# A hybrid encoder layer on one core: FFN blocks stored in two halves, squares through PSUM, the last norm rearranged

## Chip, core and metric

The kernel runs on one core of a Trainium2 chip. The metric is device time in microseconds (us) of one execution; the time before is the median of three runs. A core has TensorE (PE in the profile, its weight loads PEld), VectorE (DVE), ScalarE (ACT), GpSimd (POOL) and the queue of SyncE (SP), on which this kernel issues its DMAs.

## The reference

One layer over 1024 tokens (and 16 meta tokens) of width 1024, all in float32. The mixer is not touched by the change; what follows it is:

```python
def _rmsnorm(x, w):
    y = xf * lax.rsqrt(jnp.mean(xf * xf, axis=-1, keepdims=True) + RMS_EPS)
    return (y * w).astype(x.dtype)

def _swiglu(u, w_gate, w_up, w_down):
    return (jax.nn.silu(u @ w_gate) * (u @ w_up)) @ w_down

    for l in range(DEPTH):
        h = h + _mixer(_rmsnorm(h, norm_mix_w[l]), ...)
        h = h + _swiglu(_rmsnorm(h, norm_ffn_w[l]), w_ffn_gate[l], w_ffn_up[l], w_ffn_down[l])
    h = _rmsnorm(h, norm_final_w)
    return h[:, N_META:]
```

The FFN has 2816 hidden features, 11 blocks of 256.

## The kernel before

Activations lie with features on the 128 partitions and tokens along the free dimension, in tiles of 128 x 512 float32 (`slot`). A product of two float32 tiles is made of three matmuls on rounded halves: `split` has ACT cast a tile to its high half (L153) and DVE subtract that from the tile for the low half (L154); then come high x high, high x low, low x high.

Large products go through `seven` (L183): a 2 x 2 block product with seven block products instead of eight. It loads four weight pieces a11, a21, a22, a12, has POOL form their sums (L191 to L193, L207), splits each of the seven combinations as it is needed (ACT L209, DVE L210) and accumulates in a PSUM bank (matmuls on L217). The seven are worked in the order 11, t2, t3, n1, 21, t4, 22; of the weights, 11, t2, t3 and n1 need the first three pieces, 21 needs a12, and 22 needs a12 taken from t2's sum (L207). `seven_out` (L229) reads the banks: ACT takes the first (L233), DVE the others (L234 to L242).

The stages that matter here, in their order:

1. Output projection (L1208 to L1247), for two token halves c and eight feature tiles m: 24 matmuls, DVE adds the input (L1216), ACT squares the sum (L1245) and POOL adds the squares up in `ssum[c]` (L1246). In the second half the seven combinations for the FFN are formed as well (POOL's difference is L1236). After each half `norm` sums `ssum` over partitions with small matmuls (L1197), takes square root (ACT, L1201) and reciprocal (DVE, L1202) and spreads the factor over partitions by matmul (L174) and an ACT copy to `rs2_b` (L177).
2. Gate and up, 11 blocks j: two `seven` products, 84 matmuls each. Gate results are scaled by `rs2_b` (DVE L1257, POOL L1260 and L1262) and go through Silu (L1261); up results are multiplied in (L1267). For j < 9 the four result tiles are combined to seven (POOL L1282 and L1283, DVE L1284 and L1285), and the seven are stored to `f_d` in DRAM, on SP's queue. Blocks 9 and 10 are stored as they are. For j = 0 three quarters of the first four products are made ahead.
3. Down projection, three groups g of three blocks each (DG = 3, DQ = 3): the 21 tiles of a group are loaded to `xr` (L1303) and split into 42 tiles of the pool `bt`, which holds 58. Then four `seven` products (j = 0 to 3) of 7 x 9 = 63 matmuls each, with weights `w_dq`.
4. The rest of the down projection as plain products with blocks 9 and 10, in token chunks of 512, 256 and 256; the last `norm` of each chunk; `finish` multiplies the eight result tiles by `rs2_b` (L1339; DVE five, POOL three) and stores them.

The order of instructions on each engine is made when the program is built, by a scheduler of the framework from the dependences and its own estimates; each engine, and the SP queue, then works in that order, and a DMA or an instruction that has to wait holds up what stands behind it. A tile of a pool is given out again when its last reader is done.

## Time and profile before

| | us |
|---|---|
| median of three runs | 1775.89 (1775.68 to 1776.03) |
| the profiled execution | 1780.81 |
| its span, first to last instruction | 1779.0 |
| TensorE busy | 1714.6, 8804 matmuls |
| DVE busy | 1339.0 |
| ACT busy | 861.1 |
| POOL busy | 790.1 |
| mean granted TensorE clock | 0.987 of full speed |

The span is that of the profiled execution, which took 4.9 us longer than the median run; times in the views count from the span's start. Matmuls are pipelined and their ends are modelled, so a matmul shows 0.39 us while one begins every 0.23. Idle time of an engine stands in brackets ahead of what ended it.

### The profile page before, as it was taken

The page shows a single profiled execution, that of the slowest core. Times are in us where ns is not written, and L with a number is a line of the kernel's source. Part 1 is how long each engine was busy: PE and PEld are TensorE (multiplying, and loading weights), DVE is VectorE, ACT ScalarE, POOL GpSimd, SP SyncE. Part 2 cuts the span into 40 slices and gives each one's busy share as a digit, 9 for nine tenths or more (in the row PEclk, how much of TensorE's full clock was granted, in tenths as well). Part 3 has the DMA queues.
Part 4 walks back from the last instruction along what each step waited for, and adds up shares of the span by engine and source line. Part 5 has one row for each costly group of instructions (what it writes and reads, how often), then busy time and mean ns, then how long its engine had stood idle before and what let it go on. Part 6 is the DMA issues. An engine that isn't in the chain of part 4 may idle for free.

```text
span 1779.0 us, 26433 instructions
## 1 busy us (share of the span) xinstructions
PE 1714.6 (96%) x8804; PEld 1443.9 (81%) x8804; DVE 1339.0 (75%) x2448; ACT 861.1 (48%) x1614; POOL 790.1 (44%) x605
## 2 busy tenths in 40 slices
PE   8999999999999899999999999899999999999997
PEld 6788777788887677899998888788888888787787
DVE  7845778788888857888888758767666666987965
ACT  7425766344324523788787346433332232543434
POOL 1322257674554321234332524666676566533422
PEclk9999999999999899999999999999999999999999
DMA  7733823566546785111112754233323333854512
GB/s 255 240 101 119 295 85 117 180 201 213 189 158 230 213 301 179 28 34 40 30 59 69 231 187 162 66 101 119 101 95 101 107 105 101 286 176 123 154 57 95
DMA packets 145433, 253.59 MB, mean 143 GB/s; under 512 B 18889, under 2 KB 36738, under 8 KB 145298
## 3 DMA queue, kind: packets, MB, share of 16 engines
q1 hardware_dynamic: 145298, 251.92, 43.5%
q8 instruction: 69, 1.13, 0.3%
q14 instruction: 66, 0.54, 0.1%
HBM read 174.93 MB, written 76.85 MB: 142 GB/s over the span
## 4 chain that ended last, share of the span: by engine, by line
PE 49%; DVE 7%; DMA 3%; ACT 3%; issue 2%; SPq 0%; POOL 0%; DVEq 0%; ACTq 0%; POOLq 0%
PE mm L217 29%; PE o L1041 3%; PE mm L138 3%; PE mm L137 3%; PE mm L139 3%; PE t L1012 2%; DVE slot L154 2%; PE s L137 1%; PE s L138 1%; PE s L139 1%; DMA slot<-g_d 1%; DMA slot<-f_d 1%; DVE slot L210 1%; DVE ptl L1015 1%; PE o L137 1%
## 5 line engine op out<-in xcount | busy, mean ns | idle before, releaser
L217 PE MATMUL mm<-slot,slot 128*128 128x512 f32 x2604 | 598.3, 392 | 8.4 <-ACT slot L209 3.7
L217 PEld LDWEIGHTS mm<-slot,slot 128*128 128x128 f32 x2604 | 490.6, 189 | 115.0 <-DVE slot L210 5.5
L209 ACT CAST slot<-slot 128x512 fp32r<-128x512 f32 (+1 forms) x413 | 246.1, 598 | 465.9 <-PE mm L217 395.0
L210 DVE TENSOR_TENSOR slot<-slot,slot 128x512 fp32r<-128x512 f32 (+1 forms) x413 | 361.6, 877 | 71.5 <-ACT slot L209 70.4
L217 PE MATMUL mm<-ht,slot 128*128 128x512 f32 x648 | 219.6, 400 | 7.4 <-DVE slot L210 3.4
L217 PE MATMUL mm<-h,slot 128*128 128x512 f32 x536 | 184.4, 403 | 0.0
L191 POOL TENSOR_TENSOR slot<-slot,slot 128x512 f32<-128x512 f32 (+1 forms) x61 | 85.3, 1398 | 220.0 <-DMA slot<-in_w_u 50.7
L207 POOL TENSOR_TENSOR slot<-slot,slot 128x512 f32<-128x512 f32 (+1 forms) x61 | 84.7, 1390 | 185.1 <-DVE slot L210 173.1
L217 PEld LDWEIGHTS mm<-ht,slot 128*128 128x128 f32 x648 | 122.1, 190 | 35.1 <-DVE slot L210 5.6
L154 DVE TENSOR_TENSOR slot<-slot,slot 128x512 fp32r<-128x512 f32 x137 | 117.5, 872 | 20.6 <-ACT slot L153 20.0
L217 PE MATMUL mm<-lt,slot 128*128 128x512 f32 x324 | 128.7, 397 | 0.0
L153 ACT CAST slot<-slot 128x512 fp32r<-128x512 f32 x137 | 83.3, 619 | 76.9 <-DMA slot<-f_d 30.3
L192 POOL TENSOR_TENSOR slot<-slot,slot 128x512 f32<-128x512 f32 (+1 forms) x61 | 86.0, 1410 | 77.6 <-DVE slot L210 65.6
L217 PEld LDWEIGHTS mm<-h,slot 128*128 128x128 f32 x536 | 101.2, 190 | 21.6 <-DVE slot L210 0.6
L1002 DVE TENSOR_SCALAR_CACHE_REDUCE pr<-s,sq_c 128x384 f32<-128x384 f32 (+1 forms) x192 | 103.3, 573 | 7.9 <-PE t L1020 3.8
L217 PE MATMUL mm<-l,slot 128*128 128x512 f32 x268 | 106.6, 398 | 0.0
L139 PE MATMUL mm<-slot,slot 128*128 128x512 f32 (+1 forms) x288 | 105.3, 366 | 0.0
L138 PE MATMUL mm<-slot,slot 128*128 128x512 f32 (+1 forms) x288 | 105.3, 366 | 0.0
L137 PE MATMUL mm<-slot,slot 128*128 128x512 f32 (+1 forms) x288 | 105.1, 367 | 0.0
L1015 DVE TENSOR_TENSOR ptl<-t,pth 128x512 fp32r<-128x512 f32 x128 | 85.7, 685 | 18.2 <-ACT pth L1014 17.6
L1046 POOL TENSOR_TENSOR oa<-oa,ob 64x256 f32<-64x256 f32 x32 | 24.0, 751 | 154.5 <-ACT ob L1045 149.1
L193 POOL TENSOR_TENSOR slot<-slot,slot 128x512 f32<-128x512 f32 (+1 forms) x61 | 88.2, 1445 | 1.4
(365 smaller groups left out, 3506.0 us busy)
## 6 DMA issues: line engine op xcount, KB each, us to landing
slot<-in_w_in SPq DMA_DIRECT2D x106, 256.0 KB
f_d<-slot SPq DMA_DIRECT2D x71, 256.0 KB
slot<-f_d SPq DMA_DIRECT2D x71, 256.0 KB
slot<-in_xT SPq DMA_DIRECT2D x48, 256.0 KB
slot<-z_d SPq DMA_DIRECT2D x44, 256.0 KB
slot<-in_w_g SPq DMA_DIRECT2D x44, 256.0 KB
slot<-in_w_u SPq DMA_DIRECT2D x44, 256.0 KB
slot<-in_w_dq SPq DMA_DIRECT2D x48, 192.0 KB
```

The lines of the kernel that those rows point to most:

```text
L137: pe.matmul(ps, sh, mh, start=start, stop=False)
L138: pe.matmul(ps, sh, ml, start=False, stop=False)
L139: pe.matmul(ps, sl, mh, start=False, stop=stop)
L154: dve.tensor_sub(lo, t, f(hi))
L191: pool.tensor_add(s1, a21, a22)
L192: pool.tensor_sub(s2, s1, a11)
L193: pool.tensor_sub(a21, a21, a11)
L209: act.copy(hi, side[b])
L210: dve.tensor_sub(low, side[b], f(hi))
L217: pe.matmul(ps, sw[:, ks], sx, start=begins and q == qs[0] and i == 0, stop=q == nq - 1 and i == 2, skip_group_check=True)
L1002: dve.tensor_scalar(pr[:, c], ps[:, :n], sq_c[:, qb : qb + 1], None, ALU.mult, ALU.max, accum_out=mx[:, j : j + 1])
L1015: dve.tensor_sub(pt[1][d], tp, f(pt[0])[d])
```

## The change

- `f_d` for blocks 3 to 8 holds the high halves, and a new DRAM tensor `fl_d` the low ones: in the gate and up part each of the seven tiles is cast (ACT) and subtracted (DVE, in place), and both halves are stored. Groups 1 and 2 of the down projection load the halves straight into `bt` tiles; nothing is split there. Group 0 is as before.
- In the output projection the squares go to a PSUM tile and DVE adds them up; the one difference that POOL made in the second half is DVE's.
- `norm` of the first half stands behind both halves; that of the second half behind the matmuls of the FFN that are made ahead. `seven` remembers what was made ahead.
- `norm` also returns the reciprocal's instruction and the PSUM tile that holds the spread factor. In the last chunk the six products on DVE read that tile instead of `rs2_b`, and POOL has two products instead of three. `finish` of the chunk before is issued in two parts. From the second chunk on, odd tiles are stored from ACT's queue, even ones from SP's.

```diff
+    fl_d = mk(dram, (DQ * (DG - 1), 7, P, 512), "fl_d")
...
-            done = act.copy(dst[:, s0 : s0 + w], ps[:, :w])
-        return done
+            act.copy(dst[:, s0 : s0 + w], ps[:, :w])
+        return ps
...
-            dve.reciprocal(r2c[:, bs], r2c[:, bs])
-            spread(pr_, "r3", rs2_b, r2c, list(bl))
+            done = dve.reciprocal(r2c[:, bs], r2c[:, bs])
+            return done, spread(pr_, "r3", rs2_b, r2c, list(bl))
...
-                    pool.tensor_sub(g12, g12, g22)
+                    dve.tensor_sub(g12, g12, g22)
...
-                    t = slot(xr)
+                    t = mk(pm, (P, 512), "mm")
                     act.square(t, hm)
-                    pool.tensor_add(ssum[c], ssum[c], t)
-            norm(c, slice(0, 512))
+                    dve.tensor_add(ssum[c], t, ssum[c])
+        norm(0, slice(0, 512))
...
                 for b in NAMES[:4]:
                     prod(b, range(3))
-                    rest[b] = range(3, 4)
+                norm(1, slice(0, 512))
...
+                if j < DQ:
+                    for i, t in ((1, t2), (2, v12), (3, n1), (5, t4)):
+                        store(f_d[j, i], t)
+                else:
+                    for i, t in enumerate((v11, t2, v12, n1, v21, t4, v22)):
+                        hi = slot(hr, F32R)
+                        act.copy(hi, t)
+                        dve.tensor_sub(t, t, f(hi))
+                        store(f_d[j, i], f(hi))
+                        store(fl_d[j - DQ, i], t)
...
+                    if g == 0:
+                        raw = slot(xr)
+                        load(raw, f_d[q, i])
+                        blocks[q][nm] = split(raw, bt, bt)
+                        continue
+                    blocks[q][nm] = slot(bt, F32R), slot(bt, F32R)
+                    for t, d in zip(blocks[q][nm], (f_d[g * DQ + q, i], fl_d[(g - 1) * DQ + q, i])):
+                        load(f(t), d)
...
-        def finish(lo, n):
+        def finish(lo, n, factor, some=range(KT)):
...
-                (pool if i in (2, 5, 7) else dve).tensor_mul(hm, hm, rb)
-                store(out[i, :, lo : lo + n], hm)
+                if i in ((5, 7) if last else (2, 5, 7)):
+                    pool.tensor_mul(hm, hm, rb)
+                else:
+                    dve.tensor_mul(hm, factor[:, :n] if last else rb, hm)
+                (nc.scalar.dma_start if lo and i % 2 else store)(out[i, :, lo : lo + n], hm)
...
                 if prev:
                     with tc.issue_after(added.ins):
-                        finish(*prev)
+                        finish(*prev, range(4))
+                    with tc.issue_after(inverse.ins if lo + n == S else added.ins):
+                        finish(*prev, range(4, KT))
```

Three places of the order that results. First PE at the entry to the FFN (L217 before and L220 now are matmuls of the first gate product, L1197 and L1200 the column sums of `ssum[1]`), before and then now:

```order
L217 MATMUL mm_12503<-slot_12241,slot_12505 128x512
L217 MATMUL mm_12461<-slot_11888,slot_12462 128x512
L217 MATMUL mm_12461<-slot_11889,slot_12462 128x512
L217 MATMUL mm_12461<-slot_11888,slot_12463 128x512
L217 MATMUL mm_12475<-slot_12414,slot_12476 128x512
L217 MATMUL mm_12475<-slot_12415,slot_12476 128x512
L217 MATMUL mm_12475<-slot_12414,slot_12477 128x512
L1197 MATMUL r_2788_12435<-ones_68,ssum_2447_11114 128x1 x4
L217 MATMUL mm_12489<-slot_12419,slot_12490 128x512
```

```order
L220 MATMUL mm_12491<-slot_12229,slot_12493 128x512
L1200 MATMUL r_2807_12505<-ones_68,ssum_2448_11115 128x1 x4
L220 MATMUL mm_12449<-slot_11889,slot_12450 128x512
L220 MATMUL mm_12449<-slot_11890,slot_12450 128x512
L220 MATMUL mm_12449<-slot_11889,slot_12451 128x512
L220 MATMUL mm_12463<-slot_12402,slot_12464 128x512
```

The column sums stand right behind the 36 matmuls made ahead, where 42 stood ahead of them before.

Second DVE in the gate and up part, at the end of one of the blocks 3 to 8 and the gate of the next one (L210 and L213 are weight subtractions, L234 to L236 and L237 to L239 evacuations of the gate's banks, L1297 the new subtractions), before and then now:

```order
L1285 TENSOR_TENSOR slot_13981<-slot_13794,slot_13980 128x512
L210 TENSOR_TENSOR slot_14105<-slot_13995,slot_14104 128x512
L235 TENSOR_TENSOR slot_14007<-mm_14044,slot_14006 128x512
L210 TENSOR_TENSOR slot_14126<-slot_14002,slot_14125 128x512
L236 TENSOR_TENSOR slot_14007<-slot_14007,mm_14062 128x512
```

```order
L1289 TENSOR_TENSOR slot_14010<-slot_13823,slot_14009 128x512
L213 TENSOR_TENSOR slot_14162<-slot_14052,slot_14161 128x512
L1297 TENSOR_TENSOR slot_13819<-slot_13819,slot_14015 128x512
L1297 TENSOR_TENSOR slot_14009<-slot_14009,slot_14020 128x512
L1297 TENSOR_TENSOR slot_13726<-slot_13726,slot_14025 128x512
L238 TENSOR_TENSOR slot_14064<-mm_14101,slot_14063 128x512
L1297 TENSOR_TENSOR slot_14008<-slot_14008,slot_14030 128x512
L1297 TENSOR_TENSOR slot_13823<-slot_13823,slot_14035 128x512
L1297 TENSOR_TENSOR slot_14010<-slot_14010,slot_14040 128x512
L1297 TENSOR_TENSOR slot_13727<-slot_13727,slot_14045 128x512
L213 TENSOR_TENSOR slot_14183<-slot_14059,slot_14182 128x512
L239 TENSOR_TENSOR slot_14064<-slot_14064,mm_14119 128x512
```

The seven stand ahead of the weight subtraction for the gate's product 22 and of the evacuation that frees the bank for it.

Third SP's queue in the down projection, at the loads for group 1 (L189 and L190 load weight pieces from `w_dq`, L1303 tiles to be split, L1321 halves), before, from the third to the fourth piece of the group's first product and on to the next product's, and then now, at the fourth piece:

```order
L189 DMA slot_16589<-in_w_dq 128x384
L1303 DMA slot_16533<-f_d_98 128x512
L1303 DMA slot_16539<-f_d_98 128x512
L189 DMA slot_16590<-in_w_dq 128x384
L1303 DMA slot_16545<-f_d_98 128x512
L1303 DMA slot_16551<-f_d_98 128x512
L189 DMA slot_16703<-in_w_dq 128x384
```

```order
L1321 DMA slot_16706<-f_d_98 128x512
L1321 DMA slot_16707<-fl_d_99 128x512
L1321 DMA slot_16710<-f_d_98 128x512
L1321 DMA slot_16711<-fl_d_99 128x512
L190 DMA slot_16717<-in_w_dq 128x384
L190 DMA slot_16830<-in_w_dq 128x384
L190 DMA slot_16831<-in_w_dq 128x384
```

Of the 42 loads of halves for a group, 16 stand among earlier work, and 26 stand together ahead of that fourth piece (`slot_16717`); the pieces of the next product follow it.

## Rows read from the trace of the kernel before

**Rows 1.** The page's first part: engine, busy us, share of the span, instructions.
```profile
PE 1714.6 (96%) x8804; PEld 1443.9 (81%) x8804; DVE 1339.0 (75%) x2448; ACT 861.1 (48%) x1614; POOL 790.1 (44%) x605
```

**Rows 2.** Timeline of PE at the FFN's entry: start, us, what, xcount, [idle before].
```profile
1108.39 4.70 PE L217 MATMUL mm<-slot,slot 128*128 128x512 f32 x20
1115.17 5.30 PE L217 MATMUL mm<-slot,slot 128*128 128x512 f32 x22 [2.08 <-DVE slot L210]
1123.28 1.59 PE L1197 MATMUL r<-ones,ssum 128*128 128x1 f32 x8 [2.80 <-POOL ssum L1246]
1124.73 7.01 PE L217 MATMUL mm<-slot,slot 128*128 128x512 f32 x18
```

**Rows 3.** Windows: us, PE, PEld, DVE, ACT, POOL busy, PEclk, DMA share, GB/s.
```profile
1124.00:1130.00 6.00, 6.00 (x17) 4.84 (x17) 6.00 (x8) 2.61 (x6) 2.60 (x2) 0.50 0.13 44
...
1132.00:1516.00 384.00, 384.00 (x1698) 318.15 (x1697) 259.10 (x310) 122.70 (x205) 252.98 (x171) 1.00 0.32 103
...
1612.00:1616.00 4.00, 3.69 (x11) 2.96 (x12) 4.00 (x8) 1.58 (x4) 0.00 (x0) 0.61 0.82 251
```

**Rows 4.** Timeline of PE from the FFN's end through the down projection's three groups.
```profile
1379.81 152.71 PE L217 MATMUL mm<-slot,slot 128*128 128x512 f32 x673
1533.21 13.05 PE L217 MATMUL mm<-slot,slot 128*128 128x512 f32 x53 [0.70 <-DVE slot L235]
1547.24 6.50 PE L217 MATMUL mm<-slot,slot 128*128 128x512 f32 x27 [0.98 <-DVE slot L210]
1554.11 55.14 PE L217 MATMUL mm<-slot,slot 128*128 128x512 f32 x241 [0.37 <-DVE slot L210]
1612.31 58.93 PE L217 MATMUL mm<-slot,slot 128*128 128x512 f32 x252 [3.06 <-ACT slot L209]
1671.91 0.73 PE L217 MATMUL mm<-slot,slot 128*128 128x512 f32 x2 [0.67 <-ACT slot L209]
1673.06 44.74 PE L217 MATMUL mm<-slot,slot 128*128 128x512 f32 x196 [0.41 <-DVE slot L1321]
```

**Rows 5.** Timeline of DVE at the FFN's entry.
```profile
1112.76 1.76 DVE L154 TENSOR_TENSOR slot<-slot,slot 128x512 fp32r<-128x512 f32 x1
1114.44 0.68 DVE L210 TENSOR_TENSOR slot<-slot,slot 128x512 fp32r<-128x512 f32 x1
...
1115.64 0.68 DVE L1216 TENSOR_TENSOR slot<-mm,slot 128x512 f32<-128x512 f32 x1
```

**Rows 6.** Timeline of POOL at the FFN's entry.
```profile
1112.24 1.72 POOL L1246 TENSOR_TENSOR ssum<-ssum,slot 128x512 f32<-128x512 f32 x1
...
1120.29 1.71 POOL L1236 TENSOR_TENSOR slot<-slot,slot 128x512 f32<-128x512 f32 x1
```

**Rows 7.** Timeline of DVE at the end of one FFN block, j = 4.
```profile
1315.66 1.76 DVE L1284 TENSOR_TENSOR slot<-slot,slot 128x512 f32<-128x512 f32 x1 [1.18 <-POOL slot L1282]
...
1320.26 0.68 DVE L210 TENSOR_TENSOR slot<-slot,slot 128x512 fp32r<-128x512 f32 x1
1320.86 0.67 DVE L236 TENSOR_TENSOR slot<-slot,mm 128x512 f32<-128x512 f32 x1
...
1325.83 0.69 DVE L240 TENSOR_TENSOR slot<-mm,slot 128x512 f32<-128x512 f32 x1
```

**Rows 8.** Timeline of POOL in the same block.
```profile
1321.61 1.67 POOL L1260 TENSOR_TENSOR slot<-slot,rs_b 128x512 f32<-128x512 f32 x1 [3.03 <-DVE slot L236]
```

**Rows 9.** Windows with many loads, columns as in rows 3.
```profile
8.00:24.00 16.00, 15.39 (x56) 12.50 (x57) 10.75 (x17) 11.69 (x20) 0.00 (x0) 1.00 1.04 382
1516.00:1520.00 4.00, 4.00 (x19) 3.30 (x18) 3.77 (x5) 1.77 (x3) 4.00 (x3) 1.00 0.97 326
```

**Rows 10.** Chain of waits, one load in group 1: start, us, what.
```profile
1608.50 2.76 DMA slot<-f_d
```

**Rows 11.** Timeline of DVE and of SP at the end.
```profile
1771.36 3.35 DVE L1339 TENSOR_TENSOR slot<-slot,rs_b 128x256 f32<-128x256 f32 x5 [1.21 <-ACT rs_b L177]
...
1774.40 1.79 SPq L1340 DMA_DIRECT2D out_y<-slot  x4
```

More of the change, by code (lines that the diff above doesn't have):

```diff
@@ L194, in seven @@
         side = {"11": a11, "t2": s2, "t3": a21, "n1": s1, "21": a12, "t4": a22, "22": s2}
-        banks, w, begun = {}, {}, []
+        banks, w, begun, done = {}, {}, [], set()
         def prod(b, qs=range(nq)):
             k = BANK[b]
+            qs = [q for q in qs if (b, q) not in done]
+            done.update((b, q) for q in qs)
             begins = k not in banks
@@ L1278, in build @@
                 n1, t2, t4 = [slot(hr) for _ in range(3)]
-                store(f_d[j, 0], v11)
-                store(f_d[j, 4], v21)
-                store(f_d[j, 6], v22)
+                if j < DQ:
+                    store(f_d[j, 0], v11)
+                    store(f_d[j, 4], v21)
+                    store(f_d[j, 6], v22)
                 pool.tensor_sub(n1, v11, v12)
@@ L1285, in build @@
                 dve.tensor_sub(t4, v21, t2)
-                for i, t in ((1, t2), (2, v12), (3, n1), (5, t4)):
-                    store(f_d[j, i], t)
+                if j < DQ:
+                    for i, t in ((1, t2), (2, v12), (3, n1), (5, t4)):
[7 more added lines that the diff above has]
+                        store(fl_d[j - DQ, i], t)
             else:
@@ L1301, in build @@
                 for q in range(DQ):
-                    raw = slot(xr)
-                    load(raw, f_d[g * DQ + q, i])
-                    blocks[q][nm] = split(raw, bt, bt)
+                    if g == 0:
[6 more added lines that the diff above has]
+                        load(f(t), d)
             for j in range(4):
@@ L1332, in build @@
         acc = [[acc5[m // 2]["21" if m % 2 else "11"], acc5[m // 2]["V" if m % 2 else "12"]] for m in range(KT)]
-        def finish(lo, n):
+        def finish(lo, n, factor, some=range(KT)):
             c, cs = lo // 512, slice(lo % 512, lo % 512 + n)
             rb = rs2_b[:, lo : lo + n]
-            for i in range(KT):
+            last = lo + n == S
+            for i in some:
                 hm = acc[i][c][:, cs]
-                (pool if i in (2, 5, 7) else dve).tensor_mul(hm, hm, rb)
-                store(out[i, :, lo : lo + n], hm)
+                if i in ((5, 7) if last else (2, 5, 7)):
[3 more added lines that the diff above has]
+                (nc.scalar.dma_start if lo and i % 2 else store)(out[i, :, lo : lo + n], hm)
         hid = []
```

4 lines of the change are left out of this document (2 added, 2 removed).

## The prediction

> **What bounds the kernel now.** I read the page's engine shares first. TensorE is busy 96% of the span [rows 1], so time can only come from the places where it stands or runs slowly, and the change leaves its 8804 matmuls as they are. I then went along its timeline from where the change begins, the entry into the FFN. The reader is to see three kinds of loss there.
>
> At the entry, TensorE finishes the output projection, runs 20 matmuls of the first gate block, stands 2.08 us, runs 22 more, and stands 2.80 us for the sum of squares that POOL adds up [rows 2]. Right behind that the granted clock is 0.50, the lower of its two levels (1.2 and 2.4 GHz), from 1124 to 1130 us [rows 3], and 18 matmuls take 7.01 us [rows 2]. At full clock 673 matmuls take 152.71 us [rows 4], 0.227 us each, so 18 should take 4.1: another 2.9 lost. **The entry loses 2.08 + 2.80 + 2.9 = 7.8 us.**
>
> The gate and up part runs without a gap: 384 us busy of 384 [rows 3]. In the down projection, group 0 stands three times, 0.70 + 0.98 + 0.37 = 2.05 us; group 1 stands 3.06 us in its first 40 or so matmuls; group 2 stands 0.67 + 0.41 = 1.08 us [rows 4]. After the 3.06 us the clock falls again: 11 matmuls in 3.69 us [rows 3] instead of 2.5, 1.2 us more. Groups 1 and 2 together lose 3.06 + 1.2 + 1.08 = 5.3 us.
>
> The third is the tail. The last products on DVE begin at 1771.36 and last 3.35 us, and four output stores are issued after that, until 1774.40 + 1.79 = 1776.19 [rows 11]; the span ends at 1779.0.
>
> **Entry: squares through PSUM, and no POOL.** The last projection tile is done when the gate's first matmul starts, at 1108.39 [rows 2], but DVE reads it at 1115.64: it is 7.2 us behind [rows 5]. Its operations with two SBUF inputs take 0.68 us, and 1.76 beside one of POOL's [rows 5, 6]. The change removes 18 POOL operations (14 sums, 4 differences) and puts 18 on DVE. Each costs DVE about 0.68, against the roughly 1.1 it lost to a POOL neighbour. So DVE's queue gets no longer, and by this exchange some 0.4 shorter for each; from the seven or eight in the last four column blocks I take 3 us, and the last tile is read near 1112.6 instead of 1115.64.
>
> From there four steps lead to the complete sum: scaling on ACT, then three adds on DVE, about 3.2 us. That gives 1115.8. TensorE needs it after 36 matmuls, at 1108.39 + 36 x 0.227 = 1116.6. (The sum's matmuls stand 6 earlier than before, by the order on PE above, and the difference that gated the rest at 1120.29 [rows 6] is now a 0.68 on DVE.) So neither stand remains, and without a stand nothing lowers the clock. The margin is under 1 us. I take 7.0 of the 7.8; the bounds are 7.8 and 3, the latter if the sum is still 2 us late and the clock falls as it did.
>
> **FFN blocks stored as two halves.** For six blocks (j = 3 to 8) ACT gets 7 casts, DVE 7 subtractions, SP 7 more stores. TensorE has no slack here, so what counts is who waits. DVE now works the seven ahead of a weight subtraction that stood at 1320.26 and of the evacuation that stood at 1320.86 [rows 7]; the order on DVE above shows both places. TensorE needs both when the product before has ended, which is when DVE could read it, at 1325.83 [rows 7]. The slack is 1325.8 - 1320.94 = 4.9 us. POOL's next operation waits for that same evacuation (1321.61, after 3.03 idle) [rows 8], so POOL is quiet during the seven; they follow each other every 0.6 us (1320.26, 1320.86) [rows 7], 7 x 0.61 = 4.3 us. That just fits. I take 0.1 us per block, **0.6 us lost**; bounds 0 and, at 0.88 each (between the undisturbed 0.68 and the 1.76 of a disturbed one [rows 7]), 6 x (6.2 - 4.9) = 7.8. On SP the weight load behind the stores slips by some 2.8 us. Those weights are split more than 5 us later, so I count nothing; if that cover were gone, the 2.8 would show once per block.
>
> **Down projection.** Group 0 is still split on arrival. Its waits were for DVE and ACT, which in group 0 also split group 1's blocks; these 21 splits go. I take 1.0 of 2.05 (bounds 0 and 2.05). In groups 1 and 2 the 42 splits that made DVE late go altogether. What is late next is the load. A group has 42 tiles, the pool holds 58, so 16 can come early and 26 come while the group before does its last quarter. By the order on SP above, the fourth weight piece of the new group, which its fifth product needs, stands behind all 26 on that queue, where before it stood between the raw loads.
>
> I count from the start of that quarter. 26 loads of 262 KB and two weight pieces of 197 KB are 7.21 MB. The queue moved 382 GB/s for 16 us when it was never empty [rows 9]; that gives 18.9 us. With 0.7 us to the first free tile and 2.0 us for a load's fixed part (2.76 for one [rows 10], less its transfer), the piece lands at 21.6. Cast and subtraction add 1.4 (twice 0.68), so 23.0. The fifth product is due after 63 + 36 matmuls, 22.5. So each group stands 0.5 us instead of losing 4.3 and 1.1: 5.3 - 1.0 = **4.3 us gained**. The upper bound is 5.3 (no stand). For the lower one take the 326 GB/s that the same kind of load had at 1516 to 1520 [rows 9]: 22.1 us of transfer, 3.7 us of standing, and 1.2 for the clock, in each group; 5.3 - 9.8 = -4.5. I take 382 since that stretch is long and its queue is full. The Trainium skill's page "DMA: Bandwidth & Descriptors", section Specifications, gives about 358 GB/s of HBM for a core; a stretch at 382 is above it, but by 358 the transfer would take an estimated 20.1 us, each group would stand 1.7, and the sum would be 2.4 smaller.
>
> **Tail.** Three edits act on one chain. The last reciprocal waits for three products instead of five, but ACT now issues two stores ahead of the square root, so I count nothing for it. The products read the factor in PSUM, not the copy for which DVE stood 1.21 us [rows 11]; the copy is 0.4 of that. They come to 6 on DVE; with a PSUM operand they should not be slowed by POOL, 6 x 0.35 = 2.1 instead of 3.35. The last product ends 1.6 us earlier. Of the four stores that trail it by 1.49, two remain on each queue, which saves about 0.8. **2.4 us**; bounds 0.4 (the copy alone) and 3.3.
>
> **Sum.** 7.0 - 0.6 + 1.0 + 4.3 + 2.4 = 14.1 us. The profiled execution took 1780.81, 4.9 above the median of the runs, 1775.89; it would come to 1766.7, and the median to **1761.8**.
>
> **Rivals.**
> *Late weights* (0.20). Both groups stand 3.7 and lose 1.2 to the clock: 9.8 instead of 1.0, so 1770.6. For it: the weight piece really stands behind 26 loads, and many stretches moved less than 382. Against it: those stretches had a queue that waited for DVE. The skill's page, with 358, would fall between this and the forecast.
> *The entry still waits* (0.12). POOL's four first gate operations slow DVE as before, the sum is 2 us late, the clock falls: 3 instead of 7.0, 1765.8. Against it: the margin is there on paper; for it: it is under 1 us.
> *Slower* (0.06). The seven subtractions run beside POOL at 1.76 [rows 7]: 12.3 us against a slack of 4.9, so TensorE stands 7.4 us in each of six blocks, 44 us, 1806. The forecast turns into a loss when one costs more than (4.9 + 14.7 / 6) / 7 = 1.05 us. Against it: POOL's next operation waits for what stands behind them.
>
> **How the numbers follow.** The forecast has 0.62; its own range is 1757 to 1768. A measurement of this kernel can tell about 0.2%, 3.6 us, from no change, so faster means under 1772.3. The forecast and the waiting entry lie below it, and most of the late weights: 0.62 + 0.11 + 0.14 = 0.87. No change takes 0.07, from late weights with a slow FFN; slower 0.06. The range reaches from 1756.5 to 1771, which leaves out the slow FFN and the edge of the late weights.
>
> **What would show it.** Right: no stand over 1 us around the FFN's entry and clock 1.00 there; no stand in the six blocks over 0.3 us; under 1 us in each of groups 1 and 2, and where it is, a wait for a weight cast behind DMA; the last product and last store 1.6 and 2.4 us nearer to the last matmul. Wrong: clock 0.50 in groups 1 or 2, or gaps once per block in the FFN with DVE's subtractions over 1 us.

## The result, and the profile after

The changed kernel takes 1768.11 us, the median of six runs (1764.55 to 1770.47), where the kernel before has 1776.4 beside it: a ratio of 0.9949, 95% interval 0.9936 to 0.9962. That is 8.3 us, where 14.1 were forecast. The profiled execution took 1770.47 us, with a span of 1768.7.

To see where the time went I use one measure throughout, TensorE's **loss** in a stretch: the distance from the start of each matmul to the start of the next, less the usual one (0.226 us for 512 columns, 0.118 for 256), summed up. It holds what TensorE lost by standing and by a lower clock. The stretches hold the same matmuls in every kernel.

| stretch | loss before | loss after | gain forecast | gain measured |
|---|---|---|---|---|
| entry into the FFN | 8.9 | 3.1 | 7.0 | 5.7 |
| gate and up part | 1.1 | 4.0 | -0.6 | -2.9 |
| end of the FFN and down group 0 | 4.0 | 3.9 | 1.0 | 0.1 |
| down groups 1 and 2 | 7.1 | 1.9 | 4.3 | 5.2 |
| tail: last column sum to the end of the span | 10.3 | 9.7 | 2.4 | 0.6 |
| sum | | | 14.1 | 8.7 |

The two profiled executions are 1780.81 - 1770.47 = 10.3 us apart. Of that, 1.6 lie ahead of all that the table counts: the gate's first matmul starts at 1106.78 instead of 1108.39. TensorE loses nothing in the output projection in either kernel, so these 1.6 us are not a gain of the change. The other 8.7 are the table's sum. The loss of 1.1 before, in the gate and up part, is mostly the rounding of 0.226: matmuls there follow every 0.2267 us. The difference to the 4.0 is not touched by it.

The page's first part shows the same work as before [rows 1], in less time:

```profile
PE 1707.8 (97%) x8804; PEld 1436.6 (81%) x8804; DVE 1347.7 (76%) x2467; ACT 856.1 (48%) x1614; POOL 757.2 (43%) x586
```

**Entry.** PE's timeline of the changed kernel, to be held against [rows 2]:

```profile
1106.78 8.76 PE L220 MATMUL mm<-slot,slot 128*128 128x512 f32 x36
1115.38 0.94 PE L1200 MATMUL r<-ones,ssum 128*128 128x1 f32 x8
1116.19 1.88 PE L220 MATMUL mm<-slot,slot 128*128 128x512 f32 x7
1118.23 1.42 PE L220 MATMUL mm<-slot,slot 128*128 128x512 f32 x5 [0.17 <-DVE slot L155]
1121.39 1.16 PE L175 MATMUL r<-ident,r2c 128*128 128x128 f32 x8 [1.74 <-DVE r2c L1205]
1122.31 17.97 PE L220 MATMUL mm<-slot,slot 128*128 128x512 f32 x78
```

The two old stands are gone: 36 matmuls run in one piece and the column sums follow without a wait. A new stand of 1.74 us has come 12 matmuls later, ahead of the matmuls that spread the norm's factor over the partitions (L175). ACT's and then DVE's timeline show what they wait for:

```profile
1113.67 1.75 ACT L154 CAST slot<-slot 128x512 fp32r<-128x512 f32 x3 [0.27 <-DVE slot L1237]
1119.91 0.62 ACT L154 CAST slot<-slot 128x512 fp32r<-128x512 f32 x1 [4.49 <-DVE slot L1242]
1120.43 0.26 ACT L1204 ACTIVATE r2c<-r,eps 128x4 f32<-128x4 f32 x1
```

```profile
1114.76 3.42 DVE L155 TENSOR_TENSOR slot<-slot,slot 128x512 fp32r<-128x512 f32 x2
1118.10 1.77 DVE L1242 SCALAR_TENSOR_TENSOR slot<-slot,cols,slot 128x512 f32<-128x512 f32 x1
1119.80 1.46 DVE L155 TENSOR_TENSOR slot<-slot,slot 128x512 fp32r<-128x512 f32 x2
1121.17 0.17 DVE L1205 RECIPROCAL r2c<-r2c 128x4 f32<-128x4 f32 x1
```

The column sums are done at 1116.3 and the square root (L1204) could start. It stands in ACT's queue behind one cast, and ACT idles 4.49 us because the cast's input, the last t4 block (L1242), comes late from DVE: the two subtractions ahead of it and the block itself take 1.7 to 1.8 us each, beside POOL's three sums for the next weights.

**Gate and up.** In the gates that follow the blocks j = 4 to 8 TensorE now loses something once per block: 0.2, 0.5, 0.4, 0.5 and 1.3 us. DVE's timeline at the last of them, against [rows 7]:

```profile
1463.69 1.76 DVE L1288 TENSOR_TENSOR slot<-slot,slot 128x512 f32<-128x512 f32 x1 [3.81 <-POOL slot L1286]
1465.38 0.68 DVE L237 TENSOR_TENSOR slot<-mm,slot 128x512 f32<-128x512 f32 x1
1465.98 1.19 DVE L1289 TENSOR_TENSOR slot<-slot,slot 128x512 f32<-128x512 f32 x1
1467.09 0.68 DVE L213 TENSOR_TENSOR slot<-slot,slot 128x512 fp32r<-128x512 f32 x1
1467.69 1.88 DVE L1297 TENSOR_TENSOR slot<-slot,slot 128x512 f32<-128x512 f32 x3
1469.49 0.68 DVE L238 TENSOR_TENSOR slot<-mm,slot 128x512 f32<-128x512 f32 x1
1470.10 2.48 DVE L1297 TENSOR_TENSOR slot<-slot,slot 128x512 f32<-128x512 f32 x4
1472.50 0.68 DVE L213 TENSOR_TENSOR slot<-slot,slot 128x512 fp32r<-128x512 f32 x1
1473.10 0.68 DVE L239 TENSOR_TENSOR slot<-slot,mm 128x512 f32<-128x512 f32 x1
```

The seven (L1297) run undisturbed by POOL, 0.6 us apart, as forecast. But two evacuations stand among and behind them, and TensorE waits for both: for L238 until 1470.18 (the row below), for L239 until 1473.8.

**Down projection.** PE's timeline from the wait for L238 on, against [rows 4]; the matmuls left out run without a stand:

```profile
1470.32 29.88 PE L220 MATMUL mm<-slot,slot 128*128 128x512 f32 x129 [0.72 <-DVE slot L238]
...
1528.76 13.05 PE L220 MATMUL mm<-slot,slot 128*128 128x512 f32 x53 [0.68 <-ACT slot L154]
1542.79 126.35 PE L220 MATMUL mm<-slot,slot 128*128 128x512 f32 x551 [0.98 <-DVE slot L213]
1669.91 38.16 PE L220 MATMUL mm<-slot,slot 128*128 128x512 f32 x167 [0.77 <-DVE slot L213]
```

Group 0's first two stands (0.68 and 0.98) are those of before. Group 1 has no stand long enough for a row of its own, and the granted clock stays up. Inside it there is one short one, where ACT gets the fourth weight piece:

```profile
1594.59 0.52 ACT L212 CAST slot<-slot 128x384 fp32r<-128x384 f32 x1 [1.94 <-PE mm L220]
1602.06 2.00 ACT L212 CAST slot<-slot 128x384 fp32r<-128x384 f32 x4 [6.95 <-PE mm L220]
```

ACT was idle 6.95 us and cast the piece as soon as it landed, at 1602.06, 5.3 us after SP issued it (1596.75). The matmul that needs it starts at 1602.62 and lost 0.4 us with the next one: the late piece of the forecast. The row names a matmul as releaser; that it was the load shows in a second profile of the same kernel (the run with the changed kernel again, below), on ACT's timeline:

```profile
1600.66 0.93 ACT L212 CAST slot<-slot 128x384 fp32r<-128x384 f32 x2 [6.23 <-DMA slot<-in_w_dq]
```

The piece took 5.3 us from issue to cast there too, but was in time, and TensorE lost nothing for it. Over the profiles of kernels with these halves it cost 0 to 0.6 us in a group, so that the agreement in size with the forecast's 0.5 is partly chance. Group 2's stand of 0.77 us is not that. DVE then works three weight subtractions beside POOL, 3.93 us from 1661.04 on.

**Tail.** ACT's and then DVE's timeline, against [rows 11]. The last column sum starts at 1758.97 and ends at 1759.33.

```profile
1758.23 0.38 ACTq L1361 DMA_DIRECT2D out_y<-slot  x1
1758.66 0.51 ACT L1390 ACTIVATE slot<-slot,cols 128x256 f32<-128x256 f32 x1 [0.21 <-ACT slot L1387]
1759.38 1.29 ACTq L1361 DMA_DIRECT2D out_y<-slot  x1
1760.72 0.26 ACT L1204 ACTIVATE r2c<-r,eps 128x2 f32<-128x2 f32 x1 [1.55 <-issue]
1760.74 0.92 ACTq L1361 DMA_DIRECT2D out_y<-slot  x2
1762.49 0.37 ACT L178 COPY rs_b<-r 128x256 f32<-128x256 f32 x1 [1.51 <-PE r L175]
1763.70 1.85 ACTq L1361 DMA_DIRECT2D out_y<-slot  x4
```

```profile
1761.01 0.17 DVE L1205 RECIPROCAL r2c<-r2c 128x2 f32<-128x2 f32 x1 [1.33 <-ACT r2c L1204]
...
1762.90 2.08 DVE L1360 TENSOR_TENSOR slot<-r,slot 128x256 f32<-128x256 f32 x6 [1.06 <-ACT rs_b L178]
```

The six products take 2.08 us, as forecast (2.1). They end 6.0 us after the last sum's start, though, as they did before. What they gained, 1.27 us, went to two things in front of them. The square root starts 1.4 us after the sums, because a store stands ahead of it on ACT whose issue takes 1.29 us; about 0.3 of that is a wait for its product, which ends at 1759.68. The reciprocal gives 0.65 of it back: before, it stood that long behind five products (1770.00, where the root was done at 1769.35), and now it follows the root at once. That leaves 0.7. And the factor's matmuls take 1.22 us instead of 0.71, at a granted clock of 0.50. DVE's first product still waits for ACT's copy of the factor, though it doesn't read the copy, so the 0.4 us of the forecast for that are not saved. The 0.6 us that the tail did gain are the stores: the span ends 3.7 us after the last product, 4.3 before.

### The profile page after: what moved, and what is told of

Same layout as the page of the kernel before. It is cut to its first block, busy times and chain, and to the rows that moved or that the text cites. A ratio compares the mean times of both kernels' runs of the same rounds, so it can differ in the third digit from the quotient of the medians.

```text
span 1768.7 us, 26583 instructions
## 1 busy us (share of the span) xinstructions
PE 1707.8 (97%) x8804; PEld 1436.6 (81%) x8804; DVE 1347.7 (76%) x2467; ACT 856.1 (48%) x1614; POOL 757.2 (43%) x586
## 5 line engine op out<-in xcount | busy, mean ns | idle before, releaser
L220 PE MATMUL mm<-slot,slot 128*128 128x512 f32 x2604 | 596.1, 390 | 4.1 <-DVE slot L213 1.8
L220 PEld LDWEIGHTS mm<-slot,slot 128*128 128x128 f32 x2604 | 487.0, 188 | 112.1 <-DVE slot L213 4.4
L213 DVE TENSOR_TENSOR slot<-slot,slot 128x512 fp32r<-128x512 f32 (+1 forms) x413 | 372.0, 904 | 84.9 <-ACT slot L212 80.5
L220 PE MATMUL mm<-ht,slot 128*128 128x512 f32 x648 | 219.2, 399 | 6.9 <-DVE slot L213 3.4
L192 POOL TENSOR_TENSOR slot<-slot,slot 128x512 f32<-128x512 f32 (+1 forms) x61 | 83.6, 1371 | 284.7 <-DMA slot<-in_w_g 78.1
L220 PE MATMUL mm<-h,slot 128*128 128x512 f32 x536 | 183.9, 402 | 0.0
L210 POOL TENSOR_TENSOR slot<-slot,slot 128x512 f32<-128x512 f32 (+1 forms) x61 | 80.6, 1323 | 180.1 <-DVE slot L213 135.6
L220 PEld LDWEIGHTS mm<-ht,slot 128*128 128x128 f32 x648 | 122.1, 190 | 34.2 <-DVE slot L213 5.1
L220 PE MATMUL mm<-lt,slot 128*128 128x512 f32 x324 | 128.4, 396 | 0.0
L193 POOL TENSOR_TENSOR slot<-slot,slot 128x512 f32<-128x512 f32 (+1 forms) x61 | 89.0, 1459 | 76.5 <-DVE slot L213 72.2
L220 PEld LDWEIGHTS mm<-h,slot 128*128 128x128 f32 x536 | 100.8, 189 | 21.5 <-DVE slot L213 0.6
L220 PE MATMUL mm<-l,slot 128*128 128x512 f32 x268 | 106.4, 397 | 0.0
L155 DVE TENSOR_TENSOR slot<-slot,slot 128x512 fp32r<-128x512 f32 x95 | 79.5, 857 | 11.9 <-ACT slot L154 11.1
L194 POOL TENSOR_TENSOR slot<-slot,slot 128x512 f32<-128x512 f32 (+1 forms) x61 | 87.4, 1432 | 1.4
L1017 ACT CAST pth<-t 128x512 fp32r<-128x512 f32 x128 | 71.7, 579 | 24.9 <-PE t L1015 24.7
```

The source lines that it names most:

```text
L192: pool.tensor_add(s1, a21, a22)
L193: pool.tensor_sub(s2, s1, a11)
L194: pool.tensor_sub(a21, a21, a11)
L210: pool.tensor_sub(s2, s2, a12)
L213: dve.tensor_sub(low, side[b], f(hi))
L220: pe.matmul(ps, sw[:, ks], sx, start=begins and q == qs[0] and i == 0, stop=q == nq - 1 and i == 2, skip_group_check=True)
```

## The experiments

The theory after these readings: every part does what its rows promise, and three of them meet a queue that the sum left out: a cast ahead of the square root at the entry, evacuations among the seven subtractions, two stores ahead of the square root in the tail. The rivals are named with each run. All edits are to the changed kernel. Their whole times differ by as little as the runs of one kernel do, so that losses and rows decide; the total decides only for the last group of runs.

### Tail: all stores on SP

```
-                (nc.scalar.dma_start if lo and i % 2 else store)(out[i, :, lo : lo + n], hm)
+                store(out[i, :, lo : lo + n], hm)
```

> Edit: the changed kernel with every output store back on SP's queue. Theory, the two stores on ACT's queue hold up the last square root: in the changed kernel it starts 1.4 us after the last column sum ends; here it should start within 0.1 us of it, the factor's matmuls should take 0.7 instead of 1.2 us because TensorE stands shorter ahead of them, and the stretch from the start of the last column sum to the end of the span, 9.7 us, should come down by 1.0 to 1.9, to 7.8 to 8.7, if one queue is as good for the last eight stores as two; up to 0.8 of that is given back if it isn't. Rival, the square root waits for something else and two queues are worth the 0.8 that was forecast: the square root stays 1.4 us late and the stretch is 9.7 to 10.5.

ACT's and SP's timeline of this run:

```profile
1759.68 0.26 ACT L1204 ACTIVATE r2c<-r,eps 128x2 f32<-128x2 f32 x1 [0.38 <-PE r L1202]
```

```profile
1757.67 9.34 SPq L1361 DMA_DIRECT2D out_y<-slot  x16
```

The square root starts 0.04 us after the sums end (1759.64), so the stores were what held it. The last product ends 4.65 us after the last sum's start instead of 6.0. Yet the stretch is 10.05 us, worse than 9.7 and outside the range that I gave: SP needs 9.34 us for its 16 stores, waits for their products included. From 1761.22 on they follow each other every 0.49 us up to 1767.0, 3.1 us past the last product, and the span ends 5.4 us after that product instead of 3.7. So behind these faster products the second queue saves 1.7 us, while its early stores hold the square root by 1.35. The 1.7 can't be set against the forecast's 0.8: in the kernel before, one queue behind slower products ended 4.3 us after the last one. The factor's matmuls took 1.22 us here too, after a stand of only 0.55.

### Tail: the products read the copy

```
-                    dve.tensor_mul(hm, factor[:, :n] if last else rb, hm)
+                    dve.tensor_mul(hm, rb, hm)
```

> Edit: the changed kernel with the last six products on DVE reading the factor's copy in SBUF instead of PSUM. Theory, the PSUM operand spares DVE the company of POOL and nothing else, since DVE waits for the copy in both: the first product starts within 0.05 us of the copy's end as it does now, the six take 2.9 to 4.0 us instead of 2.08, and the span ends 0.8 to 1.9 us later after the last column sum (10.5 to 11.6 instead of 9.7). Rival A, reading PSUM also saves the wait for the copy: then the first product starts 0.4 us later here, measured from the factor's last matmul. Rival B, POOL has only two products left and is no bother: the six take 2.1 to 2.5 us and the end doesn't move.

DVE's timeline:

```profile
1763.27 3.15 DVE L1360 TENSOR_TENSOR slot<-rs_b,slot 128x256 f32<-128x256 f32 x6 [0.55 <-ACT rs_b L178]
```

The six take 3.15 us instead of 2.08 and begin 0.03 us after the copy's end, as they do when they read PSUM: the theory for both. The end did not move as expected (9.7 us, as in the changed kernel), because the factor's matmuls ran in 0.71 us this time and the stores trailed by 3.1 instead of 3.7.

### Entry: the square root first

```
+                    def fourth(t7=t7, t2=t2, m=m, wc=wc):
                         dve.scalar_tensor_tensor(t2, h0[m], wc, t2, ALU.mult, ALU.subtract)
                         t7["t4"] = split(t2, bt, bt)
...
-                norm(1, slice(0, 512))
+                done = norm(1, slice(0, 512))[0]
+                with tc.issue_after(root[0].ins), tc.issue_after(done.ins):
+                    fourth()
```

> Edit: the changed kernel with the last t4 block of the FFN's input (one multiply-subtract on DVE, a cast on ACT, a subtraction on DVE) issued behind the norm's square root and reciprocal instead of ahead of them. Theory, ACT's queue holds the square root behind the cast of that block: the square root starts within 0.5 us of the column sums' end instead of 4 us later, the stand of 1.74 us ahead of the factor's matmuls goes, and the loss of TensorE from 1080 to 1140 us falls from 3.2 to about 1.5 us. Rival, DVE and ACT are simply behind there: the stand moves to the next product that needs the evacuation or the late block, and less than 0.5 us is gained.

PE's timeline, and ACT's:

```profile
1117.16 1.16 PE L175 MATMUL r<-ident,r2c 128*128 128x128 f32 x8 [0.36 <-DVE r2c L1207]
```

```profile
1113.60 0.26 ACT L1206 ACTIVATE r2c<-r,eps 128x4 f32<-128x4 f32 x1 [0.94 <-PE r L1202]
```

The square root starts right behind the sums (1112.62 + 0.95), the stand falls from 1.74 to 0.36 us, and the entry's loss from 3.1 to 1.6, as the theory had it. What is left is DVE's three subtractions beside POOL, 5.02 us, ahead of the reciprocal.

### Entry: the factor later on TensorE

```
-        post("22", v)
-        post("11", prod("21"))
...
+        if widen is None:
+            post("22", v)
+            post("11", prod("21"))
+        else:
+            post("11", prod("21"))
+            with tc.issue_after(latest[0].ins):
+                widen()
+            post("22", v)
```

(for the first gate alone; `widen` is the spread of the second norm's factor, `latest` the last matmul of product 21)

> Edit: the changed kernel with the factor's matmuls behind the 12 matmuls of the gate's fifth product instead of ahead of them (2.7 us of work). Theory, ACT is stuck behind a cast, and it also has the copy that frees the bank of the fifth product: TensorE stands ahead of the fifth product instead, 1.5 to 2.5 us, and nothing is gained (loss from 1080 to 1140 us 2.7 to 3.7, now 3.2). Rival, the place of the factor's matmuls in TensorE's queue is the cost: the stand goes and the loss falls to about 1.5 us.

```profile
1119.67 0.73 PE L222 MATMUL mm<-slot,slot 128*128 128x512 f32 x2 [1.48 <-ACT slot L236]
1120.82 4.14 PE L222 MATMUL mm<-slot,slot 128*128 128x512 f32 x10 [0.42 <-DVE slot L215]
```

On PE's timeline the stand has moved to the fifth product, which waits for the copy that ACT (L236) works behind the same cast: 1.48 and 0.42 us. The loss is 4.5, more than the expected 2.7 to 3.7, since the granted clock then fell to 0.69 (1122 to 1126 us). The place of the factor's matmuls was not the cost; ACT's queue was.

### Tail: only the last block's stores on two queues; then no copy

```
-                (nc.scalar.dma_start if lo and i % 2 else store)(out[i, :, lo : lo + n], hm)
+                (nc.scalar.dma_start if last and i % 2 else store)(out[i, :, lo : lo + n], hm)
```

> Edit: the changed kernel with the stores of the last-but-one column block on SP and only those of the last block shared between SP and ACT. Theory, the changed kernel's tail has a gain and a loss that nearly cancel: ACT's early stores hold the square root up by 0.3 to 1.4 us, and the shared queue lets the last store go 1.7 us earlier than one queue does (5.4 us from the last product to the end with one queue, 3.7 with two). Then here both are had: the square root within 0.1 us of the sums, the last product's end to the span's end 3.1 to 3.9, and the stretch from the last column sum's start to the end 8.2 to 8.8 us (before 10.45, changed 9.8, all on SP 10.2). Rival, SP's queue with 12 stores is the bound whatever ACT does: 9.3 or more.

The square root is on time and the last product ends after 4.15 us. The stretch, 9.15 us, is 0.6 better than the changed kernel's, but not the 8.2 to 8.8 of the theory: the four stores on ACT now take 3.47 us to issue (1.85 in the changed kernel), and the span ends 5.0 us after the last product. It didn't reach the rival's 9.3 either. ACT's timeline:

```profile
1758.82 3.47 ACTq L1361 DMA_DIRECT2D out_y<-slot  x4
```

Between the four, ACT's queue stands for up to 1.1 us, and the profile shows no reason for it: this cause stays open. The run after it adds this:

```
-                if i in ((5, 7) if last else (2, 5, 7)):
+                if not last and i in (2, 5, 7):
...
-            act.copy(dst[:, s0 : s0 + w], ps[:, :w])
+            if dst is not None:
+                act.copy(dst[:, s0 : s0 + w], ps[:, :w])
```

> Edit: as the run with only the last block's stores shared, and the last block's eight products all on DVE, reading the factor in PSUM; the factor's copy to SBUF isn't made. Theory, DVE's first PSUM product waits for ACT's copy because both read one PSUM bank: without the copy it starts within 0.1 us of the factor's last matmul instead of 0.43 after it. Eight products take 2.8 us instead of 2.1, so the last ends 0.2 to 0.4 us later than with the copy, and the stretch is 8.3 to 9.1. Rival, the 0.4 us are what it takes DVE to see TensorE's matmul or to get at PSUM: then the first product starts as late as before, and the last one ends 0.7 us later.

DVE's timeline without the copy:

```profile
1757.76 2.74 DVE L1361 TENSOR_TENSOR slot<-r,slot 128x256 f32<-128x256 f32 x8 [0.18 <-PE r L175]
```

The factor's last matmul ends at 1757.73, and DVE starts 0.03 us later; with the copy it was 0.44. So it was the copy that DVE waited for. The Trainium skill, page "PSUM — Partial Sum Buffer", section "PSUM bank collisions raise a hardware error", says that two engines must not access one PSUM bank in the same partitions at the same time, two reads included. The run agrees as far as it goes: both read one bank, and the wait is gone with the copy. That the bank is the reason is argued; no run puts the copy's source into another bank. The stretch is 8.6 us, inside the range. The gain over the run before (9.15 us) is not the copy's, though: the last product ends 4.44 us after the last sum's start, 0.3 later than there, and the rest of the stretch is 4.2 us instead of 5.0.

### FFN: the seven subtractions spread out

```
-                        hi = slot(hr, F32R)
-                        act.copy(hi, t)
-                        dve.tensor_sub(t, t, f(hi))
...
+                        waiting.append(halves)
...
-        dve.tensor_add(e, prod("t2", r[1]), e)
+        one(dve.tensor_add(e, prod("t2", r[1]), e))
```

(`halves` holds the cast, the subtraction and the two stores; `one` issues the next of them behind the evacuation that it is given, on four more evacuations likewise)

> Edit: the changed kernel with the seven subtractions of each split block issued one by one behind the evacuations of the next block's gate, instead of seven in a row ahead of a weight subtraction and an evacuation. Theory, TensorE's loss in the FFN (4.0 us from the second gate product of block 0 on, 1.1 before the change) is the row of seven, which in four blocks ends 0.2 to 1.2 us after TensorE needs what stands behind it: the loss falls to 1.0 to 2.0 us. Rival, DVE lacks the time wherever they stand, or the later stores hold up SP's weight loads: the loss stays at 3.5 or more, or comes back as waits for weights.

PE's timeline from block 0 on up to 1500 us, where the window ends, is one row:

```profile
1123.74 376.43 PE L220 MATMUL mm<-slot,slot 128*128 128x512 f32 x1660
```

The loss is 1.1 us, exactly that of the kernel before. The subtractions are as many, DVE does the same work, and SP's stores didn't hold up a weight load: only the place of the seven, with their casts and stores, in the queues had cost 2.9 us.

### Halves undone

The blocks of groups 1 and 2 are stored and loaded whole and split on arrival, as before the change:

```
-                    for i, t in enumerate((v11, t2, v12, n1, v21, t4, v22)):
-                        hi = slot(hr, F32R)
...
+                    raw = slot(xr)
+                    load(raw, f_d[g * DQ + q, i])
+                    blocks[q][nm] = split(raw, bt, bt)
```

> Edit: the changed kernel with all blocks stored and loaded whole and split on arrival, as before the change; entry and tail stay changed. Theory, the halves cost 2.9 us of TensorE's time in the FFN and save 5.3 in the down projection: the FFN's loss goes back to 1.0 to 1.5, that of the down projection from 5.8 to 10 to 12, and the net is 2 to 4 us slower than the changed kernel. Rival, the stalls of groups 1 and 2 came from how the blocks before them fell in time and not from the splits: the down projection's loss stays below 8.

```profile
1605.40 60.82 PE L220 MATMUL mm<-slot,slot 128*128 128x512 f32 x252 [3.01 <-DVE slot L1324]
```

On PE's timeline group 1's stand is back (3.06 in [rows 4]), and this time half clock behind it took some 3 us. The FFN's loss is 1.1, 2.9 less than in the changed kernel; that of the down projection is 13.5, 7.7 more, of which 7.1 in groups 1 and 2 (9.0 against 1.9). Net 4.8 us slower, a little above the 2 to 4 that I expected. The entry, which this edit leaves alone, lost 4.8 us in this profile instead of 3.1 and is not counted in that. So the splits on arrival were the cause of the stalls in groups 1 and 2: they come back with them.

### Together, beside the changed kernel

The changed kernel again, for the next two runs:

> No edit: the changed kernel once more, on the chip of the three runs beside it and in as many rounds, as their measure. Expected: 6 to 10.5 us faster than before (the ratio shown first was 0.9949, interval 0.9936 to 0.9962), and in the profile a loss of 3 to 4.5 us at the entry, 3.5 to 4.1 in the FFN, 5 to 7 in the down projection.

Six runs: 1767.04 us (1763.69 to 1769.13), ratio 0.9934, interval 0.9917 to 0.9952; the kernel before had 1778.62 beside it. The difference, 11.6 us, is a little above the range that I gave, its interval reaches into it. Losses: entry 2.9, gate and up 3.9, down projection 5.4. The tail took 8.5 us this time instead of 9.7, with the same program: ACT's second early store was issued in 0.34 us instead of 1.29, the square root started 1.0 us sooner, and the factor's matmuls took 0.71.

Then the edits of the square root first, the subtractions spread out and the tail without early stores and copy, in one kernel:

> Edit: the changed kernel with three of the edits tried alone, put together: the square root ahead of the last t4 block, the seven subtractions spread over the next gate, and in the tail no early store on ACT, no copy of the factor and all eight last products on DVE. Theory, the three losses lie one behind another on TensorE's path, so what each gave alone adds up: entry 1.5 us (3.1 to 1.6), FFN 2.9 (4.0 to 1.1), tail 1.1 (9.8 to 8.7 from the last column sum to the end), 5.5 together: 1762 to 1764 where the changed kernel has 1768, a ratio of 0.991 to 0.9925 to the kernel before. Rival, a stage that starts earlier meets its loads earlier, and the down projection gives back what the FFN gained: 2 to 3 us instead of 5.5, and the down projection's loss above 7.

Six runs: 1763.79 us (1759.35 to 1765.59), ratio 0.9914, interval 0.9897 to 0.9932. The median is 3.3 us below the changed kernel's beside it; the ranges overlap. The losses are 1.5 at the entry (2.9), 1.1 in gate and up (3.9) and 5.6 in the down projection (5.4), the tail 8.7 (8.5): 3.8 us less in the profiles. So entry and FFN add up as the theory says and the down projection gives nothing back; of the 1.1 us for the tail nothing shows, because the changed kernel's tail took 1.2 us less in the profile beside it than in its first one.

Last, group 0's blocks as halves too, on top of these three:

> Edit: as the three repairs, and group 0's blocks too are stored as two halves and loaded so, instead of split on arrival. Theory, group 0's stalls (3.4 us with what stands just ahead of it) are its own 21 splits on DVE, which this takes away; but 42 halves of 262 KB, 11.0 MB, then have to come while the last up block runs, and by 382 GB/s that takes 28.8 us, against 19 us of that block and 9 x 0.227 = 2 us for each product of the group's first seven. The fourth weight piece stands behind nearly all of them: TensorE then waits 3 to 8 us for it in the first product, and the run is 0 to 5 us slower than the three repairs. Rival, the loads keep up: group 0's loss falls to under 1 us, and the run is 2 to 3 us faster.

PE's timeline, and a window of the first stand (columns as in [rows 3]):

```profile
1546.76 16.59 PE L221 MATMUL mm<-slot,slot 128*128 128x512 f32 x63 [11.41 <-ACT slot L213]
1567.65 2.58 PE L221 MATMUL mm<-slot,slot 128*128 128x512 f32 x6 [4.30 <-ACT slot L213]
```

ACT's timeline at the cast that ends the first of these stands:

```profile
1546.19 0.93 ACT L213 CAST slot<-slot 128x384 fp32r<-128x384 f32 x2 [16.34 <-DMA slot<-in_w_dq]
```

```profile
1535.00:1547.00 12.00, 0.59 (x3) 0.24 (x2) 1.64 (x3) 0.81 (x2) 0.75 (x1) 0.60 1.05 392
```

1777.64 us (12 runs, 1775.97 to 1779.02), ratio 0.9998 (0.9988 to 1.0007): 13.9 us slower than the three repairs, more than the 0 to 5 that I gave. This is the mechanism of the rival *late weights*, a weight piece behind the loads of halves, from more loads and not from a lower rate. The group's 42 loads are issued from 1509.88 to 1539.3, and the fourth weight piece behind all of them, at 1541.01; TensorE stands 11.41 us for it, and 4.30 us for the next late piece, while the queue runs at 392 GB/s. My estimate had the bytes right and left out what the piece itself takes under a full queue (5.3 us) and the other transfers of the stretch. Group 0's own stands for its splits are gone, as the theory had it, and for the load the end of the FFN and group 0 lose 20.2 us instead of 4.0.

### The entry undone

Squares to SBUF and summed by POOL, the difference on POOL, and the second norm at its old place in the gate:

```
-                    dve.tensor_sub(g12, g12, g22)
+                    pool.tensor_sub(g12, g12, g22)
...
-                    t = mk(pm, (P, 512), "mm")
+                    t = slot(xr)
                     act.square(t, hm)
-                    dve.tensor_add(ssum[c], t, ssum[c])
-        norm(0, slice(0, 512))
+                    pool.tensor_add(ssum[c], ssum[c], t)
+            norm(c, slice(0, 512))
...
-                norm(1, slice(0, 512))
+                    rest[b] = range(3, 4)
```

> Edit: the changed kernel with the FFN's entry as before the change (squares to SBUF and summed by POOL, the difference g12 on POOL, the second norm behind 12 matmuls fewer of the gate's products); halves and tail stay changed. Theory, the entry is worth what the traces show: its loss goes from 3.1 back to 8 to 9.5 us, with a stand for POOL's sum and a granted clock near 0.50 behind it, and nothing else moves by over 1 us. Rival, the blocks' stores and loads had a hand in the stalls there: the loss stays below 6.

```profile
1114.15 6.90 PE L220 MATMUL mm<-slot,slot 128*128 128x512 f32 x22 [2.25 <-DVE slot L213]
1122.28 1.05 PE L1200 MATMUL r<-ones,ssum 128*128 128x1 f32 x8 [1.22 <-POOL ssum L1249]
1123.19 2.09 PE L220 MATMUL mm<-slot,slot 128*128 128x512 f32 x8
1126.82 2.56 PE L220 MATMUL mm<-slot,slot 128*128 128x512 f32 x10 [1.54 <-DVE slot L213]
```

On PE's timeline the stands for DVE and for POOL's sum are back, with half clock behind the first of them (22 matmuls in 6.90 us). The loss is 7.7 us, a little under the 8 to 9.5 expected and above the rival's 6; the FFN (4.1) and the down projection (6.4) stay within 1 us of the changed kernel's. The clock fell for a shorter time than in the kernel before. In the order that results the column sums stand behind 42 matmuls and the factor's behind 60, where the changed kernel has 36 and 48: the expectation's "behind 12 matmuls fewer" has this the wrong way round.

## Why the prediction was right in direction and too large by 5.8 us

The measured 1768.11 lies inside the range from 1756.5 to 1771, and just outside the forecast's own, 1757 to 1768. Two of the five terms, entry and groups 1 and 2, came near their size; group 0 and the tail gave a quarter of theirs or less, and the FFN lost five times its 0.6. Of the signs set down for being right, the clock of 1.00 at the entry and stands under 1 us in groups 1 and 2 came; a stand of 1.74 us at the entry and one of 0.72 in the blocks are over their marks of 1 and 0.3, and against the last column sum the last product came 0.0 and the end of the span 0.6 us nearer, not 1.6 and 2.4.

- **Entry, 7.0 forecast, 5.7 measured.** Right: the sum is complete when TensorE needs it; the last projection tile is read at 1111.47, 4.7 us after the gate's first matmul (7.2 before, 4.2 forecast). The step that failed is "So neither stand remains": it ended with the complete sum and followed neither the square root nor the reciprocal, whose reader now stands 12 matmuls behind the sums. That the clock stayed at 1.00 in the changed kernel's profile is partly luck: the same entry code lost 2.8 to 4.8 us over the profiles, 4.4 in the run with all stores on SP, where the clock fell to 0.60 from 1122 to 1126 us behind a stand of 2.04 us.
- **FFN, 0.6 forecast, 2.9 measured**, within the bounds of 0 and 7.8. The price of the seven was right (0.6 each, no POOL). The mis-sized term is the slack of 4.9 us: it was counted to 1320.94, the end of the weight subtraction of [rows 7], and not to 1321.53, the end of the evacuation behind it, which TensorE needs as well; that leaves 4.3 for 4.2 of work. In the last block, where DVE began 0.9 us later against TensorE than in the blocks before, the evacuation among the seven was late too, by 0.7 us.
- **Group 0, 1.0 forecast, 0.1 measured.** The step that failed is that its waits came from group 1's splits. They come from its own 21, on DVE ahead of its start (the run that stored them as halves has none of these stands). The loss at the third stand, 0.37 us long at 1554.11, fell only from 0.5 to 0.3.
- **Groups 1 and 2, 4.3 forecast, 5.2 measured.** The mechanism of the late weight piece was right, and its size for group 1 in this profile (0.5 and 0.4); for group 2 it was on time, and in the kernel's second profile it was on time for both. A stand that the sum does not have, DVE beside POOL, cost 0.8 in group 2. The losses before were 1.8 larger than the stands that I added up (7.1 against 5.3), those after 0.9 larger than the forecast 1.0. So the term came out too small, and luck had a part in its nearness.
- **Tail, 2.4 forecast, 0.6 measured.** The products' 2.1 us was right. The sentence "so I count nothing for it", on ACT's two stores ahead of the square root, failed: they hold the root by 1.35 us, of which the reciprocal's shorter wait gives 0.65 back. The copy's 0.4 was not saved, since DVE still waits for it; the bank that both read is the likely reason. The lower clock of the factor's matmuls, 0.5 us, stands in no term. The stores gave 0.6 of their 0.8.
- **The rivals.** *Late weights* did not happen here and does exist: with 42 loads instead of 26 ahead of the piece, and at a full rate, TensorE stood 15.7 us for it and the next one. *The entry still waits* came half true: not the sum, but the square root. The slower case did not come: POOL was quiet during the seven.

## What to carry to other kernels

Follow a moved chain to its last reader, on every queue that it crosses: each of the three losses here came from work placed ahead of a square root or an evacuation in an in-order queue: a cast whose input was late, seven subtractions, a store. When work has to go onto an engine that others wait for, issue it piecewise behind the evacuations; the same seven subtractions cost 2.9 us in a row and nothing spread out. And before a load doubles, count what stands on its queue ahead of the next weight: here the weights behind 26 tiles cost 0 to 0.6 us a group, those behind 42 cost 15.7.

## What the runs showed of the hardware

- A load under a full queue takes 5.3 us from issue to its reader (fourth weight piece, group 1), against 2.76 in [rows 10]. The queue moved 385 GB/s from 1596 to 1600 us, at the first of these, and 392 GB/s for 12 us in the run with all blocks as halves, above the 358 that the forecast set beside its own 382 from the Trainium skill.
- The issue of the same output store on ACT took 0.34, 0.72, 0.93 or 1.29 to 1.34 us in the profiles of kernels with the same tail, and the square root behind it moved with it. Some 0.3 us of the 1.29 is a wait for the store's product. The same program had 1.29 in one profile and 0.34 in another.
- The granted clock did not follow the length of a stand: the factor's matmuls in the tail took 0.71 us behind a stand of 1.93 us in one run, and 1.22 behind 0.55 in another.
- Products with an operand in PSUM keep their pace beside POOL (six in 2.08 us, beside two of POOL's products), with both in SBUF six take 3.15.
- The gate's first matmul started at 1102.95 to 1108.39 us in the profiles, in kernels whose work ahead of it is the same but for the sums of squares. In the two profiles of the changed kernel, whose spans are 2.3 us apart, it differs by 0.45.
